# GpSimd's closing: a wait for the count of landed transfers and a resetting drain, in a row-scatter kernel

## Chip, cores, metric

One core of a Trainium2 chip. The metric is device microseconds of one execution; medians are quoted where there were several executions, and all executions used for verdicts were of the fast state (granted clock 1.0 in each). A profile's span is 1.8 us shorter than the time of the same execution (831.28 for 833.09 us before), so spans are compared with spans and times with times.

Names in the profile: PE is TensorE, DVE VectorE, ACT ScalarE, POOL GpSimd and SP SyncE; a q behind the name means the engine's sequencer, and L479 is line 479 of the kernel. Both `drain()` and `dma_reset()` stand in a trace as DRAIN; the first is called the plain drain here, the second the resetting drain. "The pool" is the framework's tile pool, which guards its tiles by semaphores of its own. An increment is one step of a semaphore that a transfer counts up as it lands. An "entry" is whatever GpSimd keeps of a transfer that it issued.

## The reference

`scores` is 8 x 2048 x 2048, `values` is 8 x 2048 x 2560, both f32.

```python
best_j = np.argmax(scores, axis=2)
gathered = values[b_idx, best_j, :].copy()
out = np.zeros_like(values)
np.add.at(out, (b_idx, best_j, slice(None)), gathered)
```

A row of `values` that is nobody's argmax becomes zero, a row chosen once is copied, a row chosen n times is multiplied by n.

## The kernel before

VectorE finds the argmaxes and counts them. The rows then move by GpSimd's indirect transfers of 128 rows each: 128 copies of single rows inside DRAM (`copy_once`), 61 scatters of zeros from `zrow`, and 40 gathers into six slots of `vbig`, each scaled by ScalarE (ACT) and scattered from there. Indices beyond the tensor drop a row.

```python
vbig = consts.tile([P, NV * H], FP32)              # six slots, from a pool
...
landed = tc.alloc_semaphore("landed")
n_free = [0]

def free_running(ins):                             # counted by hand, not by the pool's semaphores
    writes_out(ins)
    tc.add_to_no_dep_group("zrow", ins.ins)
    ins.then_inc(landed, 16)
    tc.info.no_tile_sem_insts.add(ins.ins.name)
    n_free[0] += 1
...
        for k in range(MCAP):                      # 5 per batch, 8 batches
            scatter(staged[k], mi[:, k:k + 1])     # from vbig, on the pool's semaphores
...
with tc.If(more > 0):                              # rows beyond the usual room; not taken here
    ...
nc.gpsimd.drain()
```

The framework adds a closing of its own behind this: SP's waits for the pool's semaphores, a drain of each engine, a barrier, a clearing of semaphores, a second barrier.

Of the kernel before, what the change touches and what calls it, by code (L numbers as in the profile page):

```python
# [8 lines left out]
FP32 = mybir.dt.float32  # L9
# [5 lines left out]
P = 128  # L15
# [21 lines left out]
def kernel(  # L37
# [6 lines left out]
    nc = tc.nc  # L44
    B, S, S2 = scores.shape
    _, _, H = values.shape
# [5 lines left out]
    NV = 6  # L52
# [5 lines left out]
    ZCAP, MCAP = 7, 5  # L58
# [8 lines left out]
    consts = ctx.enter_context(tc.tile_pool(name="consts", bufs=1))  # L67
# [51 lines left out]
    zrow = ctx.enter_context(nc.sbuf_tensor([P, H], FP32))  # L119
    nc.scalar.copy(zrow[:], zero1[:].to_broadcast([P, H]))  # L120

    vbig = consts.tile([P, NV * H], FP32)
    nc.scalar.copy(vbig[:, NX * R * S:NV * H], zero1[:].to_broadcast([P, NV * H - NX * R * S]))

    ones_i = ctx.enter_context(nc.sbuf_tensor([P, B * NT], INT32))
# [12 lines left out]
    landed = tc.alloc_semaphore("landed")  # L138
    n_free = [0]
# [14 lines left out]
    def scatter(v, idx, note=writes_out):  # L154
        note(nc.gpsimd.indirect_dma_start(  # L155
            out=out_flat[:, :], out_offset=bass.IndirectOffsetOnAxis(ap=idx, axis=0),
            in_=v, in_offset=None, bounds_check=B * S - 1, oob_is_err=False))
# [114 lines left out]
    def value_steps(b, cnt_ps):  # L272
# [74 lines left out]
        mi = many_i[:, b * NM:(b + 1) * NM]  # L347
# [9 lines left out]
        staged = []  # L357
# [26 lines left out]
            gathers()  # L384
            zeros(range(ZHEAD))
        for k in range(MCAP):
            scatter(staged[k], mi[:, k:k + 1])
        if b > 0:
            zeros(range(ZHEAD, nz))
        assert not rest  # L390
# [3 lines left out]
    with tc.manual_schedule(engines={ET.PE, ET.DVE, ET.Activation, ET.SP}):  # L394
        pending = iter(())
        for b in range(B):
            cnt_ps = psum_c.tile([P, NT], FP32)
            for _ in count_steps(b, cnt_ps):
                next(pending, None)
            for _ in pending:  # L400
                pass
            pending = value_steps(b, cnt_ps)
            if b < 2:
                for _ in range(4):
                    next(pending)
        for _ in pending:
            pass
        full = fin.tile([1, 2], FP32)
        nc.vector.tensor_reduce(out=full[:, 0:1], in_=tots[0:1, 0, 0:B - 1], op=ALU.max, axis=mybir.AxisListType.X)
        nc.vector.tensor_reduce(out=full[:, 1:2], in_=tots[0:1, 1, :], op=ALU.max, axis=mybir.AxisListType.X)  # L410
        over = fin.tile([1, 3], FP32)
        nc.vector.tensor_single_scalar(out=over[:, 0:1], in_=full[:, 0:1], scalar=float(ZCAP * P), op=ALU.is_gt)
        nc.vector.tensor_single_scalar(out=over[:, 1:2], in_=full[:, 1:2], scalar=float(MCAP * P), op=ALU.is_gt)
        nc.vector.tensor_single_scalar(out=over[:, 2:3], in_=most[0:1, :], scalar=float(ZLAST * LE), op=ALU.is_gt)
        over_i = fin.tile([1, 1], INT32)
        nc.vector.tensor_reduce(out=over_i[:], in_=over[:], op=ALU.max, axis=mybir.AxisListType.X)
# [3 lines left out]
    with tc.If(more > 0):  # L420

        n_spilt = 0
        last = nc.gpsimd.wait_ge(landed, 16 * n_free[0])
# [26 lines left out]
                with tc.issue_after(scaled.ins):  # L450
                    scatter(zrow[:], many_i[:, i:i + 1], one_by_one)

    nc.gpsimd.drain()


# [28 lines left out]
```

## Time and profile before

| | before |
|---|---|
| time, median (three runs) | 831.68 us (831.57 to 834.0) |
| span of the profiled execution | 831.28 us |
| last transfer issued by GpSimd | 811.90 us |
| last packet, last recorded increment of a semaphore | 826.09, 826.61 us |
| end of GpSimd's long drain | 830.46 us |

The first row is timed without regard to the trace; the others are places in one trace, from its start. The distance from the last increment to the end of the span is 4.67 us: the data has landed and the kernel isn't over. The lines behind these numbers stand in the prediction.

### The profile page before, as it was taken

The numbers are of one execution on the slowest core, as the hardware profiler recorded it, in microseconds if no ns is written. First come the engines' busy times: TensorE is split into PE (matmuls) and PEld (weight loads), VectorE is DVE, ScalarE is ACT, GpSimd is POOL, SyncE is SP. The second block draws the span as 40 slices with busy tenths as digits, with TensorE's granted clock in tenths as the row PEclk, the third lists the DMA queues.
The fourth block names the chain that finished last, engine by engine and source line by source line (L and its number), as shares of the span: only waits on it lengthen the run. The fifth ranks groups of instructions, "written<-read, shape, count | busy, mean of one in ns | idle before, by whom it ended". The sixth has DMA issues, their size and how long they took to land.

```text
span 831.3 us, 2048 instructions
## 1 busy us (share of the span) xinstructions
PE 14.7 (2%) x273; PEld 14.2 (2%) x273; DVE 679.4 (82%) x794; ACT 103.0 (12%) x43; POOL 272.6 (33%) x277
## 2 busy tenths in 40 slices
PE   0000000000000000000000000000000000000000
PEld 0000000000000000000000000000000000000000
DVE  7999999999999999999999999999999995000000
ACT  3000001401310001220002300013100410320320
POOL 0000642257121260061420241500516266356360
DMA  9999999999999999999999999999999999999995
GB/s 382 429 428 429 375 423 423 424 406 423 421 427 429 426 429 425 427 429 425 425 425 430 427 428 426 422 433 424 431 422 413 424 427 421 423 427 419 424 427 221
DMA packets 48111, 347.04 MB, mean 417 GB/s; under 512 B 19014, under 2 KB 19014, under 8 KB 19014
## 3 DMA queue, kind: packets, MB, share of 16 engines
q0 software_dynamic: 38736, 212.67, 61.8%
q1 hardware_dynamic: 9360, 134.22, 38.0%
q14 instruction: 13, 0.11, 0.0%
q8 instruction: 2, 0.03, 0.0%
HBM read 354.42 MB, written 300.15 MB: 787 GB/s over the span
## 4 chain that ended last, share of the span: by engine, by line
issue 35%; DVE 30%; POOL 17%; DMA 9%; another core or an unknown queue 5%; POOLq 0%; PE 0%
DVE am L189 14%; DVE mx L188 13%; POOL out_dram L33 9%; DMA out_dram<-vbig,many_i 8%; POOL out_dram L155 6%; POOL vbig L150 2%; DVE oh_lo L198 1%; DMA vbig<-in_scores_dram 1%; DVE oh L325 1%; DVE lo L194 0%; PE l_ps L343 0%; DVE oh_hi L202 0%; POOLq L479 0%; POOLq L155 0%
## 5 line engine op out<-in xcount | busy, mean ns | idle before, releaser
L189 DVE FIND_INDEX8 am<-mx,s_tile 128x8 uint32<-128x2048 f32 x116 | 265.1, 2285 | 0.0
L188 DVE MAX8 mx<-s_tile 128x8 f32<-128x2048 f32 x116 | 264.4, 2280 | 0.0
L363 ACT ACTIVATE vbig<-vbig,many_c 128x2560 f32<-128x2560 f32 x40 | 96.7, 2428 | 692.9 <-DMA vbig<-in_values_dram,many_i 692.9
L33 POOL DMA_INDIRECT out_dram<-in_values_dram,ones_i x128 | 131.3, 1026 | 152.9 <-DVE m L296 114.8
L155 POOL DMA_INDIRECT out_dram<-vbig,many_i x40 | 39.5, 988 | 238.0 <-ACT vbig L363 237.7
L150 POOL DMA_INDIRECT vbig<-in_values_dram,many_i x40 | 41.1, 1027 | 129.1 <-DMA out_dram<-vbig,many_i 81.5
L155 POOL DMA_INDIRECT out_dram<-zrow,zero_i x61 | 59.5, 976 | 18.8 <-issue 18.8
L188 DVE MAX8 mx<-vbig 128x8 f32<-128x2048 f32 x12 | 27.4, 2281 | 4.8 <-DMA vbig<-in_scores_dram 4.8
L189 DVE FIND_INDEX8 am<-mx,vbig 128x8 uint32<-128x2048 f32 x12 | 27.4, 2285 | 0.0
L198 DVE TENSOR_TENSOR oh_lo<-lo,lane_f 128x512 bf16<-128x512 uint32 x32 | 22.2, 695 | 0.4
L325 DVE TENSOR_TENSOR oh<-lo,fill_f 128x2048 f16<-128x2048 uint32 x8 | 18.3, 2292 | 0.3
L207 PE MATMUL cnt_ps<-oh_hi,oh_lo 128*128 128x16 bf16 x128 | 8.2, 174 | 579.1 <-DVE oh_hi L202 530.6
L207 PEld LDWEIGHTS <-oh_lo 128*128 128x128 bf16 x128 | 8.4, 105 | 578.9 <-DVE oh_lo L198 549.0
L189 DVE MATCH_VALUE_LOAD am<-mx,s_tile 128x8 f32 x116 | 10.7, 92 | 4.0
L202 DVE TENSOR_TENSOR oh_hi<-hi,lane_f 128x64 bf16<-128x64 uint32 x32 | 7.0, 218 | 0.0
L194 DVE TENSOR_SCALAR lo<-am 128x4 uint32<-128x4 uint32 x32 | 5.9, 185 | 1.1
L343 PE MATMUL l_ps<-put,oh 128*128 128x32 f16 x128 | 4.7, 188 | 69.0 <-DVE put L340 69.0
L343 PEld LDWEIGHTS <-oh 128*128 128x128 f16 x128 | 4.7, 104 | 70.0 <-DVE oh L325 59.6
L196 DVE TENSOR_SCALAR hi<-am 128x4 uint32<-128x4 uint32 x32 | 5.6, 175 | 0.0
L351 DVE TENSOR_SCALAR e<-l_ps 128x32 f32<-128x32 f32 x8 | 1.5, 188 | 3.1 <-PE l_ps L343 3.1
L330 DVE TENSOR_TENSOR ez<-hi,lane_f 128x256 f16<-128x256 uint32 x8 | 3.4, 419 | 0.0
L340 DVE TENSOR_TENSOR put<-ez,row_f 128x256 f16<-128x256 f16 x8 | 3.3, 418 | 0.0
(91 smaller groups left out, 61.1 us busy)
## 6 DMA issues: line engine op xcount, KB each, us to landing
s_tile<-in_scores_dram SPq DMA_DIRECT2D x58, 2048.0 KB
vbig<-in_scores_dram SPq DMA_DIRECT2D x5, 2048.0 KB
vbig<-in_scores_dram SPq DMA_DIRECT2D x2, 1024.0 KB
out_dram<-in_values_dram,ones_i POOLq DMA_INDIRECT x128
out_dram<-zrow,zero_i POOLq DMA_INDIRECT x61
vbig<-in_values_dram,many_i POOLq DMA_INDIRECT x40
out_dram<-vbig,many_i POOLq DMA_INDIRECT x40
```

The costliest lines, as they stand in the source:

```text
L33: return eng.add_instruction(ins)
L150: note(nc.gpsimd.indirect_dma_start(out=v, out_offset=None, in_=values_flat[:, :], in_offset=bass.IndirectOffsetOnAxis(ap=idx, axis=0), bo ...
L155: note(nc.gpsimd.indirect_dma_start(out=out_flat[:, :], out_offset=bass.IndirectOffsetOnAxis(ap=idx, axis=0), in_=v, in_offset=None, bound ...
L188: nc.vector.max(out=mx[:], in_=rows)
L189: nc.vector.max_index(out=am[:, g, :], in_max=mx[:], in_values=rows)
L194: nc.vector.tensor_single_scalar(out=lo[:], in_=am[:, :, 0], scalar=P - 1, op=ALU.bitwise_and)
L198: nc.vector.tensor_tensor(out=oh_lo[:], in0=lo[:].unsqueeze(2).to_broadcast([P, G, P]), in1=lane_f[:].unsqueeze(1).to_broadcast([P, G, P]) ...
L202: nc.vector.tensor_tensor(out=oh_hi[:], in0=hi[:].unsqueeze(2).to_broadcast([P, G, NT]), in1=lane_f[:, 0:NT].unsqueeze(1).to_broadcast([P, ...
L207: nc.tensor.matmul(out=cnt_ps[:], lhsT=oh_lo[:, g, :], rhs=oh_hi[:, g, :], start=(t == 0), stop=(t == NT - 1))
L325: nc.vector.tensor_tensor(out=oh[:], in0=lo[:].unsqueeze(2).to_broadcast([P, NT, P]), in1=fill_f[:].unsqueeze(1).to_broadcast([P, NT, P]), ...
L343: nc.tensor.matmul(out=l_ps[:], lhsT=oh[:, t, :], rhs=put[:, t, :], start=(t == 0), stop=(t == NT - 1))
L363: nc.scalar.activation(out=v, in_=v, func=mybir.ActivationFunctionType.Copy, bias=0.0, scale=mc[:, k:k + 1])
```

## The change

The intent: GpSimd shall not go through its transfers with a plain drain at the end. It counts them on a semaphore, waits for the full count, and then resets what it keeps of them. For the count to be complete, the last six scatters, which nothing in the kernel waits for, have to count on it too; then the pool no longer knows when their source is free, so `vbig` leaves the pool.

```diff
-    vbig = consts.tile([P, NV * H], FP32)
+    vbig = ctx.enter_context(nc.sbuf_tensor([P, NV * H], FP32))
...
-            scatter(staged[k], mi[:, k:k + 1])
+            scatter(staged[k], mi[:, k:k + 1], writes_out if b * MCAP + k < B * MCAP - NV else free_running)
...
-    nc.gpsimd.drain()
+    last = nc.gpsimd.wait_ge(landed, 16 * n_free[0])
+    with tc.issue_after(last.ins):
+        nc.gpsimd.dma_reset()
```

## The prediction

> **What bounds the kernel now.** I read the page's slices first, then the waits, the same activity cut into stages, the instructions of the last line of the kernel (where all closing instructions are booked), and last the transfers in the final 12 us.
>
> The page's DMA rows, one character or number for each 20.8 us of the span:
>
> ```profile
> DMA  9999999999999999999999999999999999999995
> GB/s 382 429 428 429 375 423 423 424 406 423 421 427 429 426 429 425 427 429 425 425 425 430 427 428 426 422 433 424 431 422 413 424 427 421 423 427 419 424 427 221
> ```
>
> The 16 DMA engines are full in 39 of 40 slices and move about 425 GB/s; the last slice falls to half. The page totals 347.04 MB, and 347.04 MB at 425 GB/s would take 817 us (my division) of a span of 831.3. So the body is bound by transfers, and its long GpSimd waits (for instance 237.7 us for ACT's scaling of `vbig`) cost nothing while the queues stay full. Only the two ends, some 14 us together, are not bandwidth.
>
> The stages at the end, in the view that sums each engine's busy time over stretches. Columns: stretch, its length, busy time of PE, weight load, DVE, ACT and POOL with counts, granted clock, DMA share, GB/s:
>
> ```profile
> 150.00:800.00 650.00, 12.42 (x231) 11.87 (x231) 537.88 (x644) 92.09 (x39) 231.65 (x231) 1.00 1.01 425
> 800.00:812.00 12.00, 0.00 (x0) 0.00 (x0) 0.00 (x0) 0.00 (x0) 9.16 (x10) 1.00 1.01 423
> 812.00:826.10 14.10, 0.00 (x0) 0.00 (x0) 0.00 (x0) 0.00 (x0) 0.00 (x0) 1.00 0.71 281
> 826.10:830.50 4.40, 0.00 (x0) 0.00 (x0) 0.00 (x0) 0.00 (x0) 0.00 (x0) 1.00 0.00 0
> 830.50:831.30 0.80, 0.00 (x0) 0.00 (x0) 0.00 (x0) 0.00 (x0) 0.00 (x0) 1.00 0.00 0
> ```
>
> Four phases: GpSimd issues its last scatters until 812 us; the backlog lands until 826.1; then 4.4 us in which no engine works and no byte moves; then 0.8 us of closing. The change aims at the third row. What fills it stands among the instructions booked on the kernel's last line (count, then duration in ns as minimum/median/maximum, then first and last start in us):
>
> ```profile
> L479 POOLq DRAIN  x3: 40/113/21461, 809.0 to 831.0; - x3
> L479 SPq DRAIN  x3: 7/7/7, 821.8 to 830.7; - x3
> L479 POOLq EVENT_SEMAPHORE  x4: 17/17/17, 830.5 to 831.2; - x4
> L479 POOLq EVENT_SEMAPHORE_RANGE_CLEAR  x1: 158/158/158, 830.8 to 830.8; - x1
> ```
>
> GpSimd's drain starts at 809.00 us and takes 21.461 us, so it ends at 830.46. Two more drains after it take 113 and 40 ns. SP is long done and waits for exactly this, 8.9 us of it, in the view of who waited for whom (total, times, longest):
>
> ```profile
> SPq L479 <- PEq L479: 9.4, 2, 8.9
> ```
>
> (PE's sequencer is only the name which that wait is given; PE has been idle since 697 us. The barrier is complete when GpSimd reaches it.) Was the drain waiting for data all that time? The transfers from 820 to 832 us, in 40 slices of 0.3 us:
>
> ```profile
> DMA  7575664635304210000000000000000000000000
> ```
>
> The last packet ends at 826.09 and the last semaphore increment that the trace records is at 826.61, 0.52 us later. The drain ends 830.46 - 826.61 = 3.85 us after that. These 3.85 us are what the change can take away: nothing in the trace is outstanding any more, and the drain still runs.
>
> **What the skill says.** The Trainium skill, DMA: Bandwidth & Descriptors, section "Why a DMA increments its semaphore by 16 and not by 1", says that all 16 engines post their part of a GpSimd transfer's increment, and warns that a semaphore shared by transfers in flight can pass an intermediate count too early, while the full count means that all has landed. Here the wait is for the full total, so sharing is safe. The trace records 2,897 increments of `landed` where 189 x 16 = 3,024 are due; the missing 4% are lost records, so the last landing could be a little later than 826.61. The same page, "Anatomy of one DMA", puts about 2 us of fixed cost on a transfer, mostly the write receipt; here the receipt of the last one is 0.52 us, and the change keeps it, since a counted wait needs it as much as a drain. Perfetto Trace Analysis, "Sequencer-only Instruction (DRAIN, etc)", says that the record of such an instruction covers execution and not the semaphore wait before it. This drain's 21.46 us are therefore its own execution: it started when the instruction before it was done, and polled or walked. I found no page that says what a resetting drain costs.
>
> **The change part by part.**
>
> The plain drain goes: -21.46 us of GpSimd's queue, of which all up to 826.61 lies beside transfers that have to land anyway. On the path: -3.85 us.
>
> A wait for 16 x 195 increments comes: 189 transfers are counted now (128 + 61 in the page's issue table), and 6 of the 40 scatters from `vbig` join. The records of other waits on GpSimd take 17 ns, and the closing ones follow one another by some 80 ns. I put 0.06 us from the landing to the wait's end.
>
> The resetting drain comes: it has every landed entry to forget. Plain drains with nothing to wait for took 40, 113 and 189 ns in this trace (the last at the start of the program). I choose 0.3 us, an estimate: above these since the bookkeeping of up to 269 transfers may be there, far below 3.85[...]. If the old 3.85 us were a walk over all 269 (128 + 61 + 40 + 40), it would be 14 ns each; a reset that drops them in one go doesn't pay that.
>
> The closing barrier stays: 831.28 - 830.46 = 0.82 us.
>
> The last six scatters change their semaphore. The gathers and scatters through `vbig` take eight transfer semaphores in turn, and these six leave that turn; nothing reuses their slots of `vbig`, because there are six slots and they are the last six users. SP's closing waits for these semaphores ended by 821.8, 9 us early, so taking them out is worth nothing. Turning `vbig` from a pool tile into a plain tensor is what makes this legal at the pool's release; it adds no instruction and moves no byte. `zero_i`, `ones_i` and `many_i` are plain tensors already, written and read slice by slice, and the transfers stay full, so I take it that slices of `vbig` are tracked as before.
>
> Sum of the span: 826.61 + 0.06 + 0.30 + 0.82 = 827.79 us, against 831.28, so -3.49. On the median of the timed runs: 831.68 - 3.49 = 828.2 us, that is 0.42% less.
>
> **Rivals.**
>
> First, the walk stays. If the 3.85 us are the cost of visiting ring entries and the resetting drain has to visit them too, the time stays at 831.5 to 831.9. For it: the old drain's execution goes on although the trace shows nothing in flight, so its cost is not waiting.[...] A partial walk, 1 to 2 us, would make 829 to 830.
>
> Second, the plain drain that follows at the barrier (113 ns now) inherits the work: it finds something after the reset that it must go through. That would show as a long drain in the closing, and again about 831.[...]
>
> Third, the 3.85 us are a landing that the trace has lost, and the count comes only near 830. Against it: no packet moves after 826.09, and receipts of the last packets come within about half a microsecond. It would leave 831.
>
> Fourth, the rearranged semaphores or the plain `vbig` make GpSimd wait more between gathers and scatters. The scatters of the last stage each wait for ACT and ACT for the gather; a coarser dependence on `vbig` as a whole would serialize them. If only that stage grew, the backlog (14 us at 812) would hide most; if it hit all 40 gathers, tens of us could be lost. Unlikely, as other plain tensors are handled in slices.
>
> More than 3.85 us can't be won: the data ends where it does, because no transfer, size or order of issue is touched, and GpSimd's issue times before 812 us are set by the same waits.
>
> **Range and chances.** Most of my weight (three in four) lies on a reset drain of 0.04 to 1 us: 827.9 to 828.9. One in eight is on a partial or whole walk, the rest on noise and small shifts in the last transfers: the tail hangs on the slowest DMA engine, whose last rows take 0.38 us each, and the kernel's own three runs span 831.57 to 834.0. So 828.2, range 827.4 to 830.6. Since 2% would be 16.6 us, which is more than the whole time after the last issue except the landing itself, the verdict is "within 2%" at 0.97; 0.01 for faster, 0.02 for slower (the coarse dependence).
>
> **What would show it.** Right: the last packet still ends near 826.1; a wait on GpSimd ends within 0.2 us of the last increment; then a GpSimd drain of well under 1 us; the stretch without transfers or work shrinks from 4.4 us to about 1; the closing keeps its 0.8 us. DMA share and GB/s in the body are unchanged. Wrong: a resetting drain of over 1 us, a later drain of microseconds, a wait that ends microseconds after the last packet, or new GpSimd waits for transfers into or out of `vbig` with DMA slices below 9 in the body.

## The result, and the profile after

| | before | after |
|---|---|---|
| time, first comparison (four runs each) | 831.87 us | 828.47 us (827.9 to 828.69) |
| ratio of fast runs, 95% interval | | 0.9953, 0.9935 to 0.9970 |
| last packet, last increment | 826.09, 826.61 | 824.68, 825.67 |
| from the last increment to the end of the span | 4.67 us | 1.21 us |

A ratio is the mean time of one kernel's fast runs over the mean of the other's of the same rounds, so it isn't quite the ratio of the medians quoted. The gain of about 0.4% is clear of noise.

The page of the kernel after has the same full transfers (one character or number for each fortieth of the span):

```profile
DMA  9999999999999999999999999999999999999997
GB/s 380 430 426 430 372 423 422 425 411 422 423 425 428 428 427 430 425 427 427 429 424 426 426 430 430 422 429 426 427 426 423 424 427 422 425 424 424 422 427 295
```

Of the DMA digits only the last has changed, from 5 to 7. The end in stages (stretch, length, busy time of PE, weight load, DVE, ACT, POOL, clock, DMA share, GB/s), cut at the last packet, at the start of the resetting drain and at its end:

```profile
812.00:824.70 12.70, 0.00 (x0) 0.00 (x0) 0.00 (x0) 0.00 (x0) 0.00 (x0) 1.00 0.72 286
824.70:825.70 1.00, 0.00 (x0) 0.00 (x0) 0.00 (x0) 0.00 (x0) 0.00 (x0) 1.00 0.00 0
825.70:826.00 0.30, 0.00 (x0) 0.00 (x0) 0.00 (x0) 0.00 (x0) 0.00 (x0) 1.00 0.00 0
826.00:826.90 0.90, 0.00 (x0) 0.00 (x0) 0.00 (x0) 0.00 (x0) 0.00 (x0) 1.00 0.00 0
```

The empty stretch between the last packet and the closing, 4.4 us before, is 1.3 us now. The instructions of the kernel's line with the reset (count, ns as minimum/median/maximum, first and last start in us):

```profile
L456 POOLq DRAIN  x1: 299/299/299, 825.7 to 825.7; - x1
```

and of the closing line, which was the 479th before:

```profile
L482 POOLq DRAIN  x3: 40/53/94, 826.0 to 826.6; - x3
L482 SPq DRAIN  x3: 7/7/7, 808.8 to 826.3; - x3
L482 POOLq EVENT_SEMAPHORE  x4: 17/17/17, 826.1 to 826.8; - x4
L482 POOLq EVENT_SEMAPHORE_RANGE_CLEAR  x1: 159/159/159, 826.4 to 826.4; - x1
```

Three plain drains stood on the closing line before, of 21,461, 113 and 40 ns. Three stand there now, of 53, 94 and 40 ns. So the long drain was not removed; it is still there and finds nothing to do. That corrects a reading of mine. The line `nc.gpsimd.drain()` that the diff deletes is somewhere else in the trace of the kernel before, in the list of its instructions:

```profile
L453 POOLq DRAIN  x1: 911/911/911, 0.9 to 0.9; - x1
```

It waits for no semaphore, and it stands at the start of the program, before any transfer of GpSimd's. The drain that costs time belongs to the framework's closing.

SP's waits for the pool's semaphores end by 808.8 instead of 821.8 us (the six late scatters left them), and SP then stands at the barrier for longer:

```profile
SPq L482 <- PEq L482: 17.9, 2, 17.4
```

That is worth nothing, since GpSimd reaches the barrier last in both.

### The profile page after: what moved, and what is told of

Read it like the earlier page. It is cut to its first block, busy times and chain, and to the rows that moved or that the text cites. A ratio compares the mean times of both kernels' runs of the same rounds, so it can differ in the third digit from the quotient of the medians.

```text
span 826.9 us, 2079 instructions
## 1 busy us (share of the span) xinstructions
PE 14.7 (2%) x273; PEld 14.2 (2%) x273; DVE 679.3 (82%) x794; ACT 103.0 (12%) x43; POOL 274.1 (33%) x277
## 4 chain that ended last, share of the span: by engine, by line
DVE 43%; DMA 18%; issue 17%; POOL 11%; another core or an unknown queue 8%; PE 0%; POOLq 0%
DVE am L189 19%; DVE mx L188 18%; DMA vbig<-in_values_dram,many_i 14%; POOL out_dram L33 6%; DMA out_dram<-vbig,many_i 4%; POOL out_dram L155 4%; POOL vbig L150 2%; DVE oh_lo L198 1%; DVE oh L325 1%; DMA vbig<-in_scores_dram 1%; DVE lo L194 0%; DVE oh_hi L202 0%; PE l_ps L343 0%; DVE put L340 0%
```

## The experiments

After the result, three accounts of the 3.85 us between the last increment and the end of the old drain were open. "Walk": a plain drain goes through the entries of its transfers once all have landed, and would cost the same after a counted wait. "Slack": the drain polls transfers in flight and notices late, and would be short after a counted wait. "Overlapped walk": the drain works through entries while it waits, and the 3.85 us are only the rest. Twelve kernels were run; those with a single execution are of unknown state, and their traces are what is used of them. The diffs are against the changed kernel unless the text names another. The last increment is the last one that the trace records; it moved between 825.2 and 828.0 us among the runs that do the full work without a stop in the middle, with no relation to the edit, so the tables count from it.

### The changed kernel again (a0_again)

No edit.

> The changed kernel once more, for a sharper interval and for the same chip's comparison. Both theories (walk, and late landing): 0.9945 to 0.9970 of before, a resetting drain of 0.25 to 0.35 us starting within 0.1 us of the last landing.

829.63 us against 832.19, ratio 0.9960 (0.9946 to 0.9974). The resetting drain starts at 826.686, 0.024 us after the last increment, and takes 299 ns again. As expected.

### The wait alone (a1_wait_only)

```diff
     last = nc.gpsimd.wait_ge(landed, 16 * n_free[0])
-    with tc.issue_after(last.ins):
-        nc.gpsimd.dma_reset()
```

> The wait for the count stays, the resetting drain goes; the plain drain of the closing is then the first to meet the ring entries. Theory 'walk' (the plain drain goes through every entry once everything has landed, about 14 ns for each of 269): the closing drain starts at the last landing and takes 3.5 to 4.3 us, the time is that of before, 0.998 to 1.002. Rival 'slack' (the 3.85 us come from polling transfers in flight, or from a landing that the trace lost): everything has landed when the drain starts, so it takes under 0.3 us and the time is that of the changed kernel, 0.9945 to 0.9970. Rival 'overlapped walk' (in the kernel before, part of the walk ran beside the landings): the drain takes 5 to 8 us and the time is above before, 1.001 to 1.006.

837.54 us, ratio 1.0055 (1.0041 to 1.0068): slower than before. GpSimd's instructions on its closing line:

```profile
L480 POOLq DRAIN  x3: 40/108/7675, 827.1 to 835.3; - x3
L480 POOLq COMPARE_BRANCH  x1: 43/43/43, 826.9 to 826.9; - x1
```

The wait sits on the branch at 826.91, right after the last increment at 826.89; the drain behind it starts at 827.08 with everything landed (all 3,120 increments of the count are in this trace) and still takes 7.675 us. So the cost is work and not waiting ("slack" falls), and it is twice the 3.852 us seen before: if the work is the same in both, half of it ran beside the landings in the kernel before. "Walk" in my first form, the same 3.85 us wherever it stands, falls too; the account "overlapped walk" gave 5 to 8 us and 1.001 to 1.006, and holds. One half of the change, taken alone, makes the kernel slower; all of its gain comes from the reset.

### The reset ahead of the landings (a2_reset_first)

```diff
-    last = nc.gpsimd.wait_ge(landed, 16 * n_free[0])
-    with tc.issue_after(last.ins):
+    first = nc.gpsimd.wait_ge(landed, 16)
+    with tc.issue_after(first.ins):
         nc.gpsimd.dma_reset()
+    nc.sync.wait_ge(landed, 16 * n_free[0])
```

> GpSimd waits for one transfer's worth of the count only (long landed) and resets while some 12 transfers are still under way; SP waits for the full count instead. If the resetting drain truly waits for nothing: it stands at 809 to 812 us with 0.2 to 0.5 us, the closing drain takes under 0.15 us, SP's wait ends at the last landing, and the span is 0.2 to 0.4 us shorter than the changed kernel's, ratio to before 0.9940 to 0.9970. Rival: the resetting drain waits for what is in flight; then it lasts until about 826 us and the span is the changed kernel's within 0.1 us, or longer.

829.90 us, ratio 0.9962 (0.9948 to 0.9977), correct. The reset:

```profile
L456 POOLq DRAIN  x1: 3131/3131/3131, 810.6 to 810.6; - x1
```

It ends at 813.685. The last landing is at 828.018, so it waits for no landing. It does wait for GpSimd's last two transfers to be issued (the last issue ends at 813.376) and then takes 0.31 us, as in the next run (issue ends at 812.118, reset at 812.425); I had not thought of that in the 0.2 to 0.5 us. The gain didn't come: from the last increment to the end of the span it is 1.68 us, against 1.21. SP's instructions on the closing line show why:

```profile
L483 SPq EVENT_SEMAPHORE  x12: 17/28/28, 828.2 to 829.6; - x12
L483 SPq COMPARE_BRANCH  x1: 38/38/38, 828.0 to 828.0; - x1
```

SP's wait for the count sits on the branch at 828.03, and SP's ten waits of the closing follow it in the queue from 828.20 to 828.82. They used to run early, beside the landings.

### The same, with ACT waiting (a4_reset_first_act)

```diff
-    nc.sync.wait_ge(landed, 16 * n_free[0])
+    nc.scalar.wait_ge(landed, 16 * n_free[0])
```

> As the kernel that resets before the landings, with ACT waiting for the full count in place of SP, whose own closing waits (10 of some 65 ns) stood behind it and ate the gain. From the last landing to the end of the span: 0.80 to 0.95 us against 1.21 us in the changed kernel. Time 0.3 us less than the changed kernel, which the timed runs can hardly show: ratio to before 0.9935 to 0.9970.

828.87 us against 832.31, ratio 0.9964 (0.9950 to 0.9977). ACT's instructions on the closing line:

```profile
L483 ACTq DRAIN  x2: 8/8/8, 826.2 to 826.5; - x2
L483 ACTq COMPARE_BRANCH  x1: 33/33/33, 826.0 to 826.0; - x1
```

From the last increment (826.015) to the end of the span (826.987) it is 0.97 us: 0.24 less than in the changed kernel, a little short of the 0.26 to 0.41 that I expected. The ratio can't be told from the changed kernel's 0.9960. It is the shortest ending of all kernels, and not shown to be faster.

### The semaphores as before, with wait and reset (a3_old_sems)

```diff
-    vbig = ctx.enter_context(nc.sbuf_tensor([P, NV * H], FP32))
+    vbig = consts.tile([P, NV * H], FP32)
...
-            scatter(staged[k], mi[:, k:k + 1], writes_out if b * MCAP + k < B * MCAP - NV else free_running)
+            scatter(staged[k], mi[:, k:k + 1])
```

> The semaphore part of the change undone: vbig is a pool tile again, the last six scatters count on the pool's own semaphores (SP waits for them), GpSimd waits for 189 transfers and resets. My step says that this part is worth nothing: 0.9945 to 0.9970 of before, SP's waits for these six end 4 us or more before the last landing. Rival (the shared count or the plain tensor is where some of the gain comes from): the ratio is nearer 1, 0.998 or more.

829.21 us, ratio 0.9960 (0.9946 to 0.9975), the same as the changed kernel's; correct. SP's waits end at 821.2, 4.1 us ahead of the last increment at 825.29, and the resetting drain takes 299 ns. So moving the six scatters is worth no time. It makes the count complete by itself; here SP's waits cover the six as well.

### The kernel before without its drain line (b0_no_drain_line)

```diff
-    nc.gpsimd.drain()
```

> The kernel before without its drain line at all. In its trace the line's own drain stands at 0.9 us, at the start of the program, and the 21 us drain is booked on the closing line. If that reading holds: nothing changes, the closing drain still starts near 809 us and ends 3.6 to 4.1 us after the last landing, time 831 to 834. Rival (the line is the closing drain): the drain of 21 us is gone and the time falls to about 828.

831.69 us beside 831.64 of the kernel before on the same chip, one run each (state unknown). The closing line of this kernel:

```profile
L478 POOLq DRAIN  x3: 40/113/21099, 808.0 to 829.6; - x3
```

The long drain is still there. It ends at 829.066, and the last increment is at 825.214: 3.852 us, the same number to the nanosecond as in the kernel before. Here all 3,024 increments of the count are recorded (2,897 were before), so the 3.852 us are no landing that the trace lost.

### Fewer transfers under a plain drain, alone and beside the landings (c1_no_zero_rows, c2_no_single_rows, d1_before_no_zeros)

The first two are the kernel with the wait alone, less one kind of transfer; the third is the kernel before, less the same kind as the first. All three give a wrong result.

```diff
 c1_no_zero_rows and d1_before_no_zeros:
-                scatter(zrow[:], zi[:, k:k + 1], free_running)
 c2_no_single_rows:
-            free_running(scatter_rows_in_dram(
-                nc, out_flat[:, :], values[b, t * P:(t + 1) * P, :], one_i[:, t:t + 1], last_row))
+            pass
```

> The wait without reset, where the plain drain took 7.675 us for 269 transfers (28.5 ns each), now without the 61 scatters of zeros (wrong result on purpose): 208 transfers. Cost by the transfer since the last drain: 5.7 to 6.2 us. Cost by a ring of fixed size, or only by those landed late: 7.0 us or more. Fixed cost: 7.7.

> The same without the 128 copies of single rows (wrong result on purpose): 141 transfers. By the transfer: 3.8 to 4.3 us. Ring of fixed size or fixed cost: 7.0 us or more.

> The kernel before (plain drain that starts while transfers land, no counted wait), without the scatters of zeros (wrong result on purpose). With the counted wait ahead this set took 9.145 us. In the kernel before the part after the last landing was 3.852 us in both traces, half of 7.675. If the drain makes two passes of equal cost and only the first can run beside the landings: 4.4 to 4.7 us after the last landing. If the drain retires what has landed as it goes, and only late ones are left: another share, below 3 us or above 6 us.

The closing drains, one kernel after the other in this order:

```profile
L479 POOLq DRAIN  x3: 40/107/9145, 743.6 to 753.3; - x3
```

```profile
L479 POOLq DRAIN  x3: 44/108/3506, 755.8 to 759.9; - x3
```

```profile
L478 POOLq DRAIN  x3: 40/108/18251, 730.4 to 749.2; - x3
```

With 208 transfers the drain takes 9.145 us, more than with 269; with 141 it takes 3.506, less than the 4.0 that would be in proportion to 7.675 for 269. Cost in proportion to the transfers issued is refuted by the first; a fixed cost, and a ring that is simply full at the end (7.0 us or more in both), by the second. In the third kernel the last increment is at 744.054 and the drain ends at 748.641: 4.587 us, half of 9.145 (0.502), as 3.852 is half of 7.675 (0.502). In both sets, then, about half of the drain's work runs beside the landings and half comes after them. Two passes over the entries, of which only the first overlaps, would give this; the trace doesn't show passes, only the halves.

### A plain drain in the middle (c3_mid_drain, e1_early_drain, e2_late_drain)

The wait alone, and one more drain behind the newest counted transfer after batch 4, 2 or 6. A first form, with a counted wait ahead of the middle drain (later transfers could meet the count), was not run. `newest[0]` is the transfer counted last; the lines that keep it are left out.

```diff
         assert not rest
+        if b == 3:                       # e1_early_drain: 1, e2_late_drain: 5
+            with tc.issue_after(newest[0].ins):
+                nc.gpsimd.drain()
         yield
```

> The wait without reset, all 269 transfers, and one plain drain in the middle, after the scatters of the fourth batch, with some 137 transfers after it. If the walk goes over what has been issued since the last drain: 3.6 to 4.3 us at the end. If over all that the program ever issued: 7.5 to 7.9. The time itself may rise, as GpSimd stands still in the middle.

> As the kernel with a plain drain in the middle, but the drain comes after the second batch, so some 200 transfers follow it. So far, after the last landing: 141 since the middle drain took 3.904 us, 208 took 9.145 us, 269 took 7.675 us. If the cost grows faster than the count (exponent about 2.3 from 141 and 208): 7.5 to 9.5 us, as much as or more than with 269. If it is linear in the count at 28 ns: 5.4 to 6.0 us. If what counts is the kind of transfer (without zeros is dear): also about 5.5.

> The same with the drain after the sixth batch: some 70 transfers follow. Growing faster than the count: 0.5 to 1.2 us. Linear at 28 ns: 1.9 to 2.3 us.

All are correct and slow, 853.60, 856.97 and 864.79 us, since GpSimd stands still in the middle. What counts is the closing drain:

```profile
L485 POOLq DRAIN  x3: 46/108/3904, 847.1 to 851.5; - x3
```

```profile
L485 POOLq DRAIN  x3: 46/108/9212, 845.1 to 854.9; - x3
```

```profile
L485 POOLq DRAIN  x3: 46/108/5864, 856.3 to 862.7; - x3
```

All six closing drains that started with everything landed, by the number of transfers since the drain before (for the three of this section, the transfers that GpSimd issued after the middle drain had ended in the trace):

| transfers since the last drain | kernel | closing drain, us |
|---|---|---|
| 71 | e2_late_drain | 5.864 |
| 137 | c3_mid_drain | 3.904 |
| 141 | c2_no_single_rows | 3.506 |
| 203 | e1_early_drain | 9.212 |
| 208 | c1_no_zero_rows | 9.145 |
| 269 | a1_wait_only | 7.675 |

An earlier drain changes what the last one costs, and in two of three kernels it takes work off it (3.904 and 5.864 against 7.675; but 9.212 in e1_early_drain). That fits a drain that goes through what was not yet forgotten. But 71 transfers cost more than 137. The accounts that I had written down for the last two kernels fall: linear with both, by the kind of transfer with e1_early_drain (9.212 for about 5.5), and faster than linear, which met its 7.5 to 9.5 us there, with e2_late_drain (5.864 for 0.5 to 1.2). A saw would fit: if an entry costs 5.864 / 71 = 83 ns, the six drains went through 71, 47, 42, 112, 111 and 93 entries, that is, 0, 90, 99, 91, 97 and 176 had been forgotten on the way: none, one lot of 90 to 99, or two lots of 88. GpSimd would then retire landed entries in bulk each time that its ring is full. This account was made after the numbers and no run was made to test it; no instruction in the traces has been identified as such a bulk step.

The traces hold three more drains that the table leaves out: the middle drains themselves (c3_mid_drain, e1_early_drain, e2_late_drain in this order). They start with transfers in flight, like the long drain of the kernel before.

```profile
L396 POOLq DRAIN  x1: 63966/63966/63966, 476.9 to 476.9; - x1
```

```profile
L396 POOLq DRAIN  x1: 73023/73023/73023, 235.1 to 235.1; - x1
```

```profile
L396 POOLq DRAIN  x1: 40726/40726/40726, 671.4 to 671.4; - x1
```

They end 1.725, 2.745 and 4.420 us after the last landing before their end, with 132, 66 and 198 transfers issued before. If half of the work comes after the landings and an entry costs 83 ns, 66 entries give 2.73 us (measured 2.745); with one lot of 90 or 91 forgotten, the 42 left of 132 give 1.73 (measured 1.725) and the 107 left of 198 give 4.42 (measured 4.420). The lots of the closing drains of c3_mid_drain and e1_early_drain were 90 and 91 too. So the halves and the saw hold for three drains from which they were not made, in kernels that differ only in where that drain stands. What GpSimd does in a lot, and when, stays open.

## Why the prediction was right

828.2 us was predicted and 828.47 measured, in the range. By its steps:

- **The path.** "More than 3.85 us can't be won", said the prediction, since the data ends where it does. The span fell by 4.41 us, but 0.94 of it is the last increment, which came earlier (825.67 for 826.61) and wanders from run to run: in the kernel without its drain line it was at 825.21. From the last increment to the end it fell from 4.67 to 1.21, by 3.47 us; my sum was 3.49. The profiled execution of before, whose time was 833.09, was simply a long one; the median of the rounds fell by 3.40.
- **The wait.** 0.06 us predicted, 0.024 measured from the last increment to the start of the reset. Perfetto Trace Analysis, section "Sequencer-only Instruction (DRAIN, etc)", of the Trainium skill says that the record starts when the semaphores are satisfied; the trace agrees for this instruction, since the resetting drain carries the wait itself and its record starts 0.024 us behind the last increment, not at 809. It does not for all (see the last section).
- **The resetting drain.** 0.30 us estimated, 0.299 measured in all three runs that waited first. That so exact a hit came from an estimate between 0.19 and 3.85 us is luck in the digit; the prediction took it as given that a reset drops its entries in one go, which no trace had shown. What is shown is that the reset doesn't go through the 7.675 us of work, and, by the reset that ended 14 us ahead of the last landing, that it doesn't wait for landings.
- **The closing.** 0.82 predicted, 0.88 measured, because the closing's own drain (53 ns) now stands in it.
- **The semaphores and `vbig`.** Nothing predicted; undone, they change nothing (0.9960 either way).
- **The rivals.** None came about. The third, a lost landing, falls with the complete record of the kernel without its drain line. The second, that the plain drain behind inherits the work, had the structure right: that drain is the very one that was long, and the reset left it 53 ns.

Two steps were wrong without harm to the number. "The plain drain goes" took the deleted line for the long drain; the line ran at 0.9 us and deleting it alone does nothing. Its 911 ns were in the trace, and the prediction's list of plain drains (40, 113 and 189 ns) passes them over. And "14 ns each" for all 269 transfers was a mis-sized term: the full work is 7.675 us, half of it hidden before, and it doesn't follow the number of transfers issued. A slip besides: the stretch that "the change aims at" is the fourth row of the prediction's table of stages, not the third. Had the change been only the wait, the sum would have said "nothing", and the kernel was 0.55% slower.

## What to carry to other kernels

Measure the ending from the last landing: time between it and the end of the span moves no data, and here 3.47 of 4.67 us could be removed although the body is full of transfers. A counted wait ahead of a plain drain took away the overlap that the drain had and made this kernel slower; it paid only with a reset, which left the drain 53 ns. And see in the trace where an instruction without dependences really went before reasoning about its removal.

## What the Trainium skill lacked or had wrong

- DMA: Bandwidth & Descriptors describes GpSimd's descriptor rings, but not that a plain drain goes on working after everything has landed: 3.5 to 9.2 us in six kernels where it began then, and about half of that where it began beside the landings (3.852 for 7.675, 4.587 for 9.145).
- No page that I found has the resetting drain: 0.30 us, also with transfers under way; it waits for GpSimd's transfers to be issued (it ended 0.31 us after the last issue) but not for their landing (14.3 us later).
- Perfetto Trace Analysis, "Sequencer-only Instruction (DRAIN, etc)", doesn't say that a drain's execution can hold the landings of transfers: GpSimd's drain ran 21.46 us with them inside its record. That a record starts only when the semaphores are satisfied held for the resetting drain (0.024 us), but not for two of SP's closing waits in the changed kernel: their records took 6.026 and 9.167 us where the others of that kind take 28 ns, and the view of waits shows 9.2 us of waiting for GpSimd there.
- DMA: Bandwidth & Descriptors, "Anatomy of one DMA", puts about 2 us of fixed cost on a transfer, mostly receipt; from the last packet of GpSimd's queue to the last recorded increment, which leaves the setup out, it was 0.33 to 1.12 us in all fourteen traces.
